# The decay's and the rate's low-rank products, issued together in the two halves of the array's rows

## The chip, the cores and the metric

The kernel runs on one core of a Trainium2 chip. Its time is the device time of one execution in microseconds (us); of several runs the median is given. The engines are TensorE (PE in the profile, PEld for its weight loads), VectorE (DVE), ScalarE (ACT), GpSimd (POOL) and SyncE (SP), which issues most of the DMAs. Each has its own queue of instructions, runs it in order, and waits on semaphores for the others.

## The reference, cut to what matters

One layer of a hybrid decoder, on 512 prompt tokens and 8 sequences of 4 sample tokens, 544 tokens in all. A combined projection feeds three branches: a gated MLP, an RWKV-7 recurrence with 16 heads of 64 channels, and cross-attention to a memory. The branches are projected, gated and summed, and an MLP follows. What is changed lies in the RWKV branch, where the projections `wl` and `al` (64 channels each) give the decay and the rate of each of 1024 channels:

```python
w_log = -jax.nn.softplus(-(p['w0'] + jnp.tanh(wl) @ p['w_w2']).astype(f32)) - 0.5
decay = jnp.exp(-jnp.exp(w_log))
a = jax.nn.sigmoid((p['a0'] + al @ p['w_a2']).astype(f32))
...
kk = heads(kz * p['k_k'])
kk = kk * lax.rsqrt(jnp.sum(kk * kk, axis=-1, keepdims=True) + 1e-12)
k = kz.astype(f32) * (1.0 + (a - 1.0) * p['k_a'].astype(f32))
...
y, S = wkv7_scan(r_h, heads(decay), k_h, v_h, -kk, kk * a_h, wkv0.astype(f32))
```

## The kernel before, in words

Channels lie on the 128 partitions and the 544 tokens along the free axis. The big products, which the text calls the trunk, are tiles of 128 output features (`trunk`, L500): eight tiles of input features with three products each, of a weight and an activation that are each split into two float32r parts. A weight half comes by DMA (L190), ACT makes its first part (`whi`, L198) and DVE its second (`wlo`, L211), two halves ahead of their use. Everything else on PE is float32, and for each such product that the program names the trace shows two passes (weight loads and matmuls).

The recurrence is done in chunks of 32 tokens, for a pair of heads (128 channels) at a time: eight pairs, `pr` 0 to 7, two of them to a group. `prep_pair` prepares a pair. The decay's product (L842) takes the 64 rows of `la` that hold `tanh(wl)`, the rate's (L849) the other 64 rows; each goes over 544 tokens as 256 and 288 columns. ACT makes them `t_L` and `t_a` by a tanh (L844, L850) and squares the keys (L843). DVE rescales `t_L` (L852), PE sums the squares by head (L859), DVE scans `t_L` (L865), PE spreads the norms (L878), DVE forms the rows `AG..e` and `AG..o` (L904, L905), and PE multiplies the rows of each chunk (L923, L925), in two quarters of the array that share neither rows nor columns. When both pairs of a group are there, POOL inverts the chunks' triangles (`inv_stream`): DVE transposes them in (L1005), POOL runs a chain of 60 instructions (L1010, L1012), DVE sets the diagonal (L1015) and transposes out (L1017, L1019), and PE uses them first at L1026. After that the recurrence itself (L1067 to L1106) steps from chunk to chunk, and `out_stream` finishes the values (`y_f` at L1158, the product with wg at L543).

Streams of such pieces are dealt out by a planner (`Sched`), which knows rough times of the instructions and no overlap on PE: a piece follows when its stream's priority and its results allow, and the trunk fills what is left. A piece ends at a `yield`; DONE means that the stream's next piece waits for this one's results. The plan fixes the order of each engine's instructions. An accumulator `pst` has two PSUM banks of 512 columns; three of them serve this stage, and `take` and `pt_free` get and return one.

Of the kernel before, what the change touches and what calls it, by code (L numbers as in the profile page):

```python
# [39 lines left out]
class Dry:  # L40
    """Stands in for a device object of which only the calls matter."""
# [17 lines left out]
class Shape:  # L59
    """Stands in for a tile or a view of one while the order of the program is planned."""  # L60
# [41 lines left out]
class Model:  # L102
    """Rough times of the engines' instructions: from these the order of the program is planned. An
    instruction waits for its engine and for what its own piece of the program has written."""
# [58 lines left out]
class Plan:  # L163
    """The order in which the streams' pieces follow each other, and the choices on the way: found
    on the model, then replayed."""
# [8 lines left out]
class Weights:  # L174
    """Streams the weight halves [128, 4 x 128] in the order of their use, splitting each into the
    two float32r parts two halves ahead of its use."""
# [17 lines left out]
    def high(self):  # L194
        """The first part of the next half."""
        hi = self.pool.tile([128, 512], F32R, name="whi")
        raw = self.pool.tile([128, 512], F32, name="wraw") if self.dry else self.raw.pop(self.nhi)
        self.nc.scalar.copy(hi, raw)  # L198
        self.his[self.nhi] = hi, raw
        self.nhi += 1  # L200
# [31 lines left out]
    def advance(self, lo):  # L232
        """Keeps the parts AHEAD halves ahead: first the one, later the other."""
        if not self.dry:
            self.load_to(self.nhi + 1)
            if self.nhi >= len(self.plan.seq) + (lo and self.nlo < self.nhi):
                return
        elif self.nhi >= HALVES_ALL + (lo and self.nlo < self.nhi):
            return
        else:  # L240
            self.nc.model.side = True
        if lo:
            self.low()
            if not self.dry:
                self.load_to(self.nhi + RAWB)
        else:
            self.high()
        if self.dry:
            self.nc.model.side = False
# [32 lines left out]
class Sched:  # L282
    """Interleaves generators by priority. What a generator yields says when its next piece should
    follow: at once (NOW), when the results of this one are there (DONE), not before a time has passed
    (AFTER, or PAUSE if without them), or when a flag has been set: ("need", flag) after the results, too, ("when", flag) without them. A run ends when only streams of the background
    are left."""
# [58 lines left out]
def body(nc, tc, io, plan, dry, dbg=None):  # L345
# [16 lines left out]
    def psum(n):  # L362
        """n accumulators of two banks and single banks for the rest."""
        if pools:
            pools["small"].close()
            pools["big"].close()
        pools["big"], pools["small"] = ExitStack(), ExitStack()
        pools["t"] = pools["big"].enter_context(tc.tile_pool(name="ps_t", bufs=1, space=PSUM))
        pools["c"] = pools["small"].enter_context(tc.tile_pool(name="ps_c", bufs=8 - 2 * n, space=PSUM))
        slots[:] = [0.0] * n  # L370

    def pt():
        """The accumulator that is free first, until pt_free."""
# [107 lines left out]
    def flush():  # L481
        """The next one of the late parts of each tile."""
# [7 lines left out]
    def trunk(key, xh, xl, evac, halves=HALVES, needs=None):  # L490
        """128 output features: eight tiles of 128 input features, three products each. evac may return
        its later parts, one or a list, and whether the accumulator is free without them."""
# [29 lines left out]
    def trunk_stream():  # L522
        """The trunk's tiles: the first job whose condition holds, of the queues in their order."""
# [13 lines left out]
    def sum_bc(lhsT, rhs, ps=None):  # L537
        """[128, 544] = lhsT^T rhs in float32."""
# [11 lines left out]
    def sum_cols(out, t, blocks=range(5)):  # L550
        """The sum over the features, over D, a token to a partition: out [128, 5]."""
# [3 lines left out]
    def spread(out, recb, blocks=range(5)):  # L555
        """The blocks' factors [128, 5, 128], one for each token, to every partition."""
# [19 lines left out]
    # =====================================================================================  # L576
    # Phase 0: memory keys and values, first norm
    # =====================================================================================
# [104 lines left out]
    # =====================================================================================  # L683
    # Phase 2: RWKV
    # =====================================================================================
# [30 lines left out]
    def shift(ps, j, t, after=None):  # L716
        """Mixes each row with the one before; two parts, the second one to be called later."""
# [66 lines left out]
    def ev_gelu(dst):  # L784
        """Twice the gelu."""
# [36 lines left out]
    def prep_pair(g, pi, d):  # L822
# [16 lines left out]
        # decay and rate of each channel  # L839
        ps, sl = yield from take()  # L840
        for o, s, n in HALVES:
            PE.matmul(ps[:, o:o + n], lhsT=wa2[0:64], rhs=la[0:64, s:s + n], start=True, stop=True)  # L842
        S.activation(sq, k, AF.Square, scale=vc("kk", pr))  # L843
        S.activation(L, ps[:, 256:800], AF.Tanh, scale=0.5, bias=hv[:, pr:pr + 1])  # L844
        pt_free(sl)
        yield DONE
        ps, sl = yield from take()
        for o, s, n in HALVES:
            PE.matmul(ps[:, o:o + n], lhsT=wa2[64:128], rhs=la[64:128, s:s + n], start=True, stop=True)  # L849
        S.activation(a, ps[:, 256:800], AF.Tanh, scale=0.5, bias=hv[:, 8 + pr:9 + pr])  # L850
        pt_free(sl)
# [3 lines left out]
        # 1 / |kk|^2 by token and head  # L855
# [33 lines left out]
        # decayed rows  # L889
# [28 lines left out]
        # products of the rows of a chunk  # L918
# [24 lines left out]
        # the sample rows' hats wait in DRAM for the sample stage  # L943
# [21 lines left out]
    def fill(g, half):  # L965
        """Values and token-major keys of half the chunks, into the tiles that the recurrence reads."""
# [29 lines left out]
    def inv_stream():  # L996
        for g in range(4):
# [3 lines left out]
            # inverses of the unit lower triangles, one matrix to a partition  # L1001
# [107 lines left out]
    def group_norm(Yt, n):  # L1109
        """Yt [128, n, 64] in place: zero mean and unit variance over the last axis."""  # L1110
# [53 lines left out]
    def slot_512():  # L1164
        """A bank that the piece at hand also empties."""
        ps, sl = yield from take()
        pt_free(sl)
        return ps[:, 0:512]
# [135 lines left out]
    # =====================================================================================  # L1304
    # Phase 3: spatial gating, attention, the branches' projections
    # =====================================================================================
# [8 lines left out]
    def pair(first, k, name):  # L1315
        """The two float32r parts of feature tile k, in the first or the second set of buffers."""
# [80 lines left out]
    def gate_in(first):  # L1397
        """Token-major values."""
# [31 lines left out]
    def layer_norm(first):  # L1430
        """The values are twice the reference's, and so is what stands under the root four times it."""
# [92 lines left out]
    def cache_stream():  # L1524
        """The cached heads [128, 2 x 256], split into their float32r parts ahead of their use."""
# [24 lines left out]
    def sample_att():  # L1550
# [4 lines left out]
        # sel[8 h + 4 l + t, 16 + 4 h + t] = 1: adds the rows of the two parts (l) of the queries  # L1555
        sel = sb(sa, [32, 48], "sel")
        # for each half of the sum, the queries (or weights) of head h of sequence b at column 24 + 32 (4 b + h),
        # in two parts, and zeros between, so that 32 columns from 8 h before them put their products at rows 8 h
        qp = sb(sa, [128, 2, 1048], "qp", F32R)

        def parts_to(x, k):
            """The two parts of x [128, 8, 4, 4] (b h t)."""
# [22 lines left out]
        def products(name, half):  # L1585
            """Four sequences' products with their four queries or weights, whose two parts stand side by
            side (rows 8 h + 4 l + t), as rows of SBUF."""
# [79 lines left out]
    def prompt_att():  # L1667
# [14 lines left out]
        for h in range(4):  # L1682
# [11 lines left out]
            # scores and softmax  # L1694
# [67 lines left out]
    # =====================================================================================  # L1762
    # Phase 4: output projection, MLP, final norm
    # =====================================================================================
# [13 lines left out]
    def square(tot, j):  # L1778
        """Adds x1[j] squared to tot."""
# [27 lines left out]
    def ev_up(c, j):  # L1807
        """The square of what is above zero; the norm's factor, which is above zero, comes after w_down."""
# [40 lines left out]
    def last_two():  # L1849
        """The last two tiles, the first tokens of both before the others of both, so that the end of the  # L1850
        first ones' work runs beside the others' products."""
# [76 lines left out]
    def final_stream(half):  # L1928
        """The final norm and the output of the first or of the other tokens."""
# [142 lines left out]
```

## Time and profile before

| | |
|---|---|
| runs shown | 1496.42, 1493.64, 1495.51 us, median 1495.51 |
| span of the profiled execution | 1494.6 us, 0.9 below that median |
| PE busy | 1419.6 us, 95% |
| DVE, ACT, POOL busy | 64%, 42%, 29% |
| mean granted clock of TensorE | 0.981 of full speed |
| the changed products | 64 passes between 102 and 535 us |

A row of the timeline has the start in us, the duration in us, the engine, line and operation, the tile written and those read, the shape and the count of instructions merged; in brackets stands how long the engine was idle before it, and for whom. A duration on PE reaches from an instruction's start to its modelled end, and successive matmuls overlap; what one costs is read from the distance between starts. Rows of the groups of instructions end in busy time, mean ns of one, and the idle time before them.

### The profile page before, as it was taken

The page shows a single profiled execution, that of the slowest core. Times are in us where ns is not written, and L with a number is a line of the kernel's source. Part 1 is how long each engine was busy: PE and PEld are TensorE (multiplying, and loading weights), DVE is VectorE, ACT ScalarE, POOL GpSimd, SP SyncE. Part 2 cuts the span into 40 slices and gives each one's busy share as a digit, 9 for nine tenths or more (in the row PEclk, how much of TensorE's full clock was granted, in tenths as well). Part 3 has the DMA queues.
Part 4 walks back from the last instruction along what each step waited for, and adds up shares of the span by engine and source line. Part 5 has one row for each costly group of instructions (what it writes and reads, how often), then busy time and mean ns, then how long its engine had stood idle before and what let it go on. Part 6 is the DMA issues. An engine that isn't in the chain of part 4 may idle for free. (4 is left out here: it accounts for less than half of the span.)

```text
span 1494.6 us, 31352 instructions
## 1 busy us (share of the span) xinstructions
PE 1419.6 (95%) x12436; PEld 1326.7 (89%) x12436; DVE 952.5 (64%) x1639; ACT 630.0 (42%) x1549; POOL 426.1 (29%) x485
## 2 busy tenths in 40 slices
PE   7899989998998899999998998999999999999997
PEld 7899988887888788878888897889999999999996
DVE  6747877757778777577657667664564454544544
ACT  4434335655565365555424145542334323323222
POOL 5320281452107503620333333322110020120222
PEclk9999999999999999999999999999999999999998
DMA  6632222222312322242467557633422222223222
GB/s 223 192 112 83 91 65 71 70 68 81 107 60 69 112 83 90 89 148 93 153 221 279 180 174 247 224 126 119 156 85 86 89 96 85 91 79 97 88 86 82
DMA packets 106499, 177.45 MB, mean 119 GB/s; under 512 B 15440, under 2 KB 29008, under 8 KB 106352
## 3 DMA queue, kind: packets, MB, share of 16 engines
q1 hardware_dynamic: 104512, 172.06, 36.0%
q8 instruction: 98, 1.61, 0.4%
q0 software_dynamic: 640, 2.23, 0.4%
q10 hardware_dynamic: 1200, 1.16, 0.2%
q14 instruction: 49, 0.40, 0.1%
HBM read 147.89 MB, written 27.51 MB: 117 GB/s over the span
## 5 line engine op out<-in xcount | busy, mean ns | idle before, releaser
L211 DVE TENSOR_TENSOR wlo<-wraw,whi 128x512 fp32r<-128x512 f32 x372 | 309.1, 848 | 44.1 <-ACT whi L198 41.5
L198 ACT CAST whi<-wraw 128x512 fp32r<-128x512 f32 x372 | 224.0, 618 | 159.3 <-PE pst L500 102.0
L500 PE MATMUL pst<-hh,whi 128*128 128x256 f32 (+1 forms) x1184 | 275.2, 314 | 9.6 <-DVE Em L985 4.5
L500 PE MATMUL pst<-hh,wlo 128*128 128x256 f32 (+1 forms) x1184 | 247.1, 290 | 2.2 <-DVE wlo L211 2.2
L500 PE MATMUL pst<-hl,whi 128*128 128x256 f32 (+1 forms) x1184 | 246.5, 290 | 0.0
L500 PEld LDWEIGHTS pst<-hh,whi 128*128 128x128 f32 x1184 | 189.2, 191 | 30.1 <-issue 10.6
L500 PEld LDWEIGHTS pst<-hh,wlo 128*128 128x128 f32 x1184 | 192.0, 191 | 2.7 <-DVE wlo L211 2.7
L500 PEld LDWEIGHTS pst<-hl,whi 128*128 128x128 f32 x1184 | 192.8, 191 | 0.0
L1837 POOL TENSOR_TENSOR x<-x,dn 128x544 f32<-128x544 f32 x24 | 41.7, 1737 | 292.8 <-DVE dn L1835 292.8
L500 PE MATMUL pst<-gh,whi 128*128 128x256 f32 (+1 forms) x512 | 106.4, 289 | 0.0
L500 PE MATMUL pst<-gl,whi 128*128 128x256 f32 (+1 forms) x512 | 105.5, 287 | 0.0
L500 PE MATMUL pst<-gh,wlo 128*128 128x256 f32 (+1 forms) x512 | 105.1, 287 | 0.0
L1090 ACT COPY YU<-psc 32x64 f32<-32x64 f32 x256 | 51.7, 202 | 76.7 <-DVE Xe L1087 71.3
L500 PE MATMUL pst<-y_h,whi 128*128 128x256 f32 (+1 forms) x384 | 83.1, 298 | 0.3 <-ACT pr L1710 0.3
L500 PEld LDWEIGHTS pst<-gl,whi 128*128 128x128 f32 x512 | 82.7, 189 | 0.0
L500 PEld LDWEIGHTS pst<-gh,whi 128*128 128x128 f32 x512 | 81.9, 188 | 0.1
L500 PEld LDWEIGHTS pst<-gh,wlo 128*128 128x128 f32 x512 | 81.7, 188 | 0.0
L1010 POOL TENSOR_TENSOR Tt<-Xinv 128x30 f32<-128x30 f32 (+14 forms) x120 | 67.9, 566 | 45.9 <-DVE Xinv L1005 37.1
L500 PE MATMUL pst<-y_l,whi 128*128 128x256 f32 (+1 forms) x384 | 79.7, 289 | 0.0
L500 PE MATMUL pst<-y_h,wlo 128*128 128x256 f32 (+1 forms) x384 | 79.6, 289 | 0.0
L1012 POOL TENSOR_TENSOR Xinv<-Xinv,Tt 128x30 f32<-128x30 f32 (+14 forms) x120 | 75.2, 627 | 9.4
L1813 DVE TENSOR_TENSOR ff_r<-ff_r,pst 128x544 f32<-128x544 f32 x32 | 23.1, 720 | 81.4 <-ACT ff_r L1812 81.4
(411 smaller groups left out, 3149.5 us busy)
## 6 DMA issues: line engine op xcount, KB each, us to landing
wraw<-win SPq DMA_DIRECT2D x148, 256.0 KB, 2.7
wraw<-up SPq DMA_DIRECT2D x64, 256.0 KB, 2.7
wraw<-down SPq DMA_DIRECT2D x64, 256.0 KB, 2.7
wraw<-br SPq DMA_DIRECT2D x48, 256.0 KB, 3.3
craw<-ck SPq DMA_DIRECT2D x32, 256.0 KB, 4.3
craw<-cv SPq DMA_DIRECT2D x32, 256.0 KB, 3.6
gz_d<-gzs SPq DMA_DIRECT2D x24, 272.0 KB, 2.9
gt<-gz_d SPq DMA_DIRECT2D x24, 272.0 KB, 3.0
```

The costliest lines, as they stand in the source:

```text
L198: self.nc.scalar.copy(hi, raw)
L211: (self.nc.gpsimd if pool else self.nc.vector).tensor_tensor(lo, raw, hi, op=ALU.subtract)
L500: PE.matmul(ps[:, o:o + n], lhsT=w[:, c], rhs=x[kt][:, s:s + n], start=kt == 0 and i == 0, stop=kt == KT - 1 and i == 2)
L1010: G.tensor_tensor(t3, X[:, j + 1:32, j:j + 1].to_broadcast([128, n, j]), X[:, j:j + 1, 0:j].to_broadcast([128, n, j]), op=ALU.mult)
L1012: G.tensor_tensor(X[:, j + 1:32, 0:j], X[:, j + 1:32, 0:j], t3, op=ALU.add)
L1090: S.copy(YU[q + 32 * pi:q + 32 * pi + 32, c, :], p3[q:q + 32, pi, :])
L1813: V.tensor_tensor(r, r, ps[:, 256:800], op=ALU.mult)
L1837: G.tensor_tensor(x1[j], x1[j], t, op=ALU.add)
```

## The change: both products in one piece, half of the tokens at a time

The two pieces for the decay and the rate become two pieces for the first and the second 272 tokens. Each issues the decay's product in rows 0 to 63 of the array and the rate's in rows 64 to 127, both over all 128 columns, into the two banks of one accumulator, and then two tanhs of 272 columns. The Square comes behind the tanhs of the first piece. The rescaling of `t_L` and `k1` become a piece of their own, behind a DONE. All other edits replace comments by blank lines, which keeps the line numbers.

```diff
-        for o, s, n in HALVES:
-            PE.matmul(ps[:, o:o + n], lhsT=wa2[0:64], rhs=la[0:64, s:s + n], start=True, stop=True)
-        S.activation(sq, k, AF.Square, scale=vc("kk", pr))
-        S.activation(L, ps[:, 256:800], AF.Tanh, scale=0.5, bias=hv[:, pr:pr + 1])
-        pt_free(sl)
-        yield DONE
-        ps, sl = yield from take()
-        for o, s, n in HALVES:
-            PE.matmul(ps[:, o:o + n], lhsT=wa2[64:128], rhs=la[64:128, s:s + n], start=True, stop=True)
-        S.activation(a, ps[:, 256:800], AF.Tanh, scale=0.5, bias=hv[:, 8 + pr:9 + pr])
-        pt_free(sl)
+        for half in range(2):
+            ps, sl = yield from take()
+            h = slice(272 * half, 272 * half + 272)
+            for q in (0, 64):
+                PE.matmul(ps[:, 8 * q:8 * q + 272], lhsT=wa2[q:q + 64], rhs=la[q:q + 64, h], start=True, stop=True)
+            S.activation(L[:, h], ps[:, 0:272], AF.Tanh, scale=0.5, bias=hv[:, pr:pr + 1])
+            S.activation(a[:, h], ps[:, 512:784], AF.Tanh, scale=0.5, bias=hv[:, 8 + pr:9 + pr])
+            pt_free(sl)
+            if half == 0:
+                S.activation(sq, k, AF.Square, scale=vc("kk", pr))
+            yield DONE
         V.tensor_scalar(L, L, -DECAY_C, -DECAY_C, op0=ALU.mult, op1=ALU.add)
         S.activation(k1, k, AF.Copy, scale=hv[:, 24 + pr:25 + pr])
         yield DONE
```

The plan comes out differently from the first pair on. On PE, at the first pair's decay (`la` holds both inputs, `wa` the pair's weights, `hh` and `whi` are the trunk's):

```order
 L500 MATMUL pst<-hh_95,wlo 128x256
 L500 MATMUL pst<-hh_95,wlo 128x288
-L842 MATMUL pst<-la,wa_1051 128x256
-L842 MATMUL pst<-la,wa_1051 128x288
+L845 MATMUL pst<-la,wa_1051 128x272 x2
 L500 MATMUL pst<-hh_96,whi 128x256
 L500 MATMUL pst<-hh_96,whi 128x288
```

Two products of the trunk's size become two of half that size, and the second such row stands 18 trunk instructions further on, where L849 stood 12 further on.

On DVE, at the end of the first group's inversion (`Xinv` is the inverse, `AG1o` the rows of the third pair), before the change:

```order
L211 TENSOR_TENSOR wlo<-wraw,whi 128x512
L1015 COPY Xinv<-qmask 128x32
L904 TENSOR_TENSOR AG1o<-t_r,PP 64x16x32
L905 SCALAR_TENSOR_TENSOR AG1o<-t_L,PP 64x16x32
L1017 STREAM_TRANSPOSE Tt<-Xinv 128x32x32
```

On the same engine and at the same place after it:

```order
L904 TENSOR_TENSOR AG1o<-t_r,PP 64x16x32
L905 SCALAR_TENSOR_TENSOR AG1o<-t_L,PP 64x16x32
L1015 COPY Xinv<-qmask 128x32
L211 TENSOR_TENSOR wlo<-wraw,whi 128x512
L1017 STREAM_TRANSPOSE Tt<-Xinv 128x32x32
```

L1015, which needs the last of POOL's chain, moves from ahead of the rows to behind them, and a weight part of the trunk comes to stand behind it.

On DVE, at the end of the second group's inversion (L1086, L1087 and L1102 belong to the recurrence's step), before the change:

```order
L1015 COPY Xinv<-qmask 128x32
L1102 TENSOR_TENSOR Xe<-psc,SP 64x2x64
L1102 TENSOR_TENSOR Xo<-psc,SP 64x2x64
L1017 STREAM_TRANSPOSE Tt<-Xinv 128x32x32
L211 TENSOR_TENSOR wlo<-wraw,whi 128x512
```

There after it (`gzs` is a gelu of the trunk's):

```order
L1015 COPY Xinv<-qmask 128x32
L1017 STREAM_TRANSPOSE Tt<-Xinv 128x32x32
L794 SCALAR_TENSOR_TENSOR gzs<-gzs,pst 128x544
L1019 STREAM_TRANSPOSE CT_1028<-Xinv 128x32x32
L211 TENSOR_TENSOR wlo<-wraw,whi 128x512
L1086 COPY Xo<-psc 32x2x64
```

The step's additions (L1102) move ahead of L1015, and its copies stand behind the transpositions.

Counted along PE's order: from the odd pair's last chunk product to the first L1026 there are 288, 258, 342 and 282 trunk instructions in the four groups before, and 294, 240, 330 and 282 after. From the first decay product to L859 there are 30, 30, 30, 18, 24, 24, 12 and 18 before, and 48, 36, 54, 24, 30, 24, 48 and 30 after. Behind the last product with wg (L543 of `out_stream`) 198 trunk instructions with w_in are left before, 162 after. The array's shape (rows x columns) changes 523 times from one product to the next before, 529 times after.

## Rows read from the trace of the kernel before

**Rows 1.** The page: busy times, and TensorE's granted clock in 40 slices, in tenths.

```profile
PE 1419.6 (95%) x12436; PEld 1326.7 (89%) x12436; DVE 952.5 (64%) x1639; ACT 630.0 (42%) x1549; POOL 426.1 (29%) x485
...
PEclk9999999999999999999999999999999999999998
```

**Rows 2.** Stretches: length, PE, PEld, DVE, ACT, POOL busy (instructions), PEclk, DMA share, GB/s.

```profile
100.00:200.00 100.00, 98.45 (x839) 93.21 (x838) 76.54 (x149) 40.98 (x101) 26.37 (x36) 1.00 0.25 78
200.00:300.00 100.00, 92.13 (x994) 82.78 (x992) 72.86 (x151) 49.66 (x152) 40.92 (x63) 0.95 0.22 69
...
500.00:600.00 100.00, 95.03 (x1059) 83.91 (x1058) 78.22 (x157) 56.52 (x166) 25.35 (x41) 0.98 0.30 97
...
1000.00:1100.00 100.00, 100.00 (x805) 100.00 (x805) 50.48 (x65) 32.92 (x57) 21.94 (x16) 1.00 0.41 128
```

**Rows 3.** Groups of PE's instructions, 100 to 540 us: the decay's and the rate's.

```profile
L842 PE MATMUL pst<-la,wa 64*128 64x256 f32 (+1 forms) x32 | 9.4, 415 | 0.0
L849 PE MATMUL pst<-la,wa 64*128 64x256 f32 (+1 forms) x32 | 9.4, 415 | 0.0
```

**Rows 4.** Timeline of PE around the first decay product.

```profile
101.88 0.41 PE L500 MATMUL pst<-hh,wlo 128*128 128x256 f32 x2
102.22 1.18 PE L842 MATMUL pst<-la,wa 64*128 64x256 f32 x4
...
103.69 0.41 PE L500 MATMUL pst<-hl,whi 128*128 128x256 f32 x2
```

**Rows 5.** Timeline of PE around a float32 product on the full array.

```profile
124.71 0.41 PE L500 MATMUL pst<-hh,wlo 128*128 128x256 f32 x2
124.96 1.08 PE L543 MATMUL pst<-t_x,bones 128*128 128x256 f32 x4
...
126.13 0.41 PE L500 MATMUL pst<-hl,whi 128*128 128x256 f32 x2
```

**Rows 6.** Timeline of PE at the first chunk products.

```profile
126.72 0.27 PE L923 MATMUL pst<-AG0e,BK 64*64 64x64 f32 x1
126.72 0.27 PE L925 MATMUL pst<-AG0o,BK 64*64 64x64 f32 x1
126.83 0.22 PE L923 MATMUL pst<-AG0e,BK 64*64 64x64 f32 x1
...
126.88 0.22 PE L923 MATMUL pst<-AG0e,BK 64*64 64x64 f32 x1
```

**Rows 7.** Timeline of PE at the third pair's chunk products.

```profile
216.95 0.32 PE L923 MATMUL pst<-AG1e,BK 64*64 64x64 f32 x2
221.14 0.36 PE L925 MATMUL pst<-AG1o,BK 64*64 64x64 f32 x1 [3.87 <-DVE AG1o L905]
221.14 0.36 PE L923 MATMUL pst<-AG1e,BK 64*64 64x64 f32 x1
```

**Rows 8.** Groups of ACT's instructions: a tanh, an exponential and a copy out of PSUM.

```profile
L844 ACT ACTIVATE t_L<-pst,hv 128x544 f32<-128x544 f32 x8 | 5.7, 709 | 4.7 <-PE pst L842 4.6
L1710 ACT ACTIVATE pr<-pst,nm 128x256 f32<-128x256 f32 x16 | 7.3, 471 | 1.3 <-DVE sms L1627 0.9 <-DVE nm L1705 0.4
L625 ACT COPY rstm<-psc x1: 372/372/372, 21.7 to 21.7; 128x256 f32<-128x256 f32 x1
```

**Rows 9.** Timeline of DVE at the end of the first inversion.

```profile
219.46 0.20 DVE L1015 COPY Xinv<-qmask 128x32 f32<-128x32 f32 x1 [6.59 <-POOL Xinv L1012]
```

**Rows 10.** A stretch behind that wait, columns as in rows 2.

```profile
220.50:230.70 10.20, 8.04 (x128) 7.50 (x130) 8.27 (x9) 1.99 (x4) 0.85 (x3) 0.50 0.25 80
```

**Rows 11.** Timelines of DVE and PE at the end of the second inversion.

```profile
321.99 2.17 DVE L1017 STREAM_TRANSPOSE Tt<-Xinv 128x1024 f32<-128x1024 f32 x1
...
326.25 1.20 PE L1026 MATMUL pst<-CT,Tt 32*32 32x32 f32 x64
```

**Rows 12.** Timelines of DVE and PE at the end of the third inversion.

```profile
503.82 2.08 DVE L1017 STREAM_TRANSPOSE Tt<-Xinv 128x1024 f32<-128x1024 f32 x1
...
506.50 1.54 PE L543 MATMUL pst<-t_x,bones 128*128 128x256 f32 x4 [2.47 <-DVE y_f L1158]
```

More of the change, by code (lines that the diff above doesn't have):

```diff
@@ L838, in prep_pair @@
         k1 = sb(rp, [128, T], "t_n")
-        ps, sl = yield from take()
-        for o, s, n in HALVES:
-            PE.matmul(ps[:, o:o + n], lhsT=wa2[0:64], rhs=la[0:64, s:s + n], start=True, stop=True)
-        S.activation(sq, k, AF.Square, scale=vc("kk", pr))
-        S.activation(L, ps[:, 256:800], AF.Tanh, scale=0.5, bias=hv[:, pr:pr + 1])
-        pt_free(sl)
-        yield DONE
-        ps, sl = yield from take()
-        for o, s, n in HALVES:
-            PE.matmul(ps[:, o:o + n], lhsT=wa2[64:128], rhs=la[64:128, s:s + n], start=True, stop=True)
-        S.activation(a, ps[:, 256:800], AF.Tanh, scale=0.5, bias=hv[:, 8 + pr:9 + pr])
-        pt_free(sl)
+        for half in range(2):
[9 more added lines that the diff above has]
+            yield DONE
         V.tensor_scalar(L, L, -DECAY_C, -DECAY_C, op0=ALU.mult, op1=ALU.add)
```

## The prediction

> **What bounds the kernel now.** I read the page first: TensorE is busy 95% of the span and holds its high clock nearly throughout [rows 1]. A table by stretches shows where that is not so: behind 1000 us PE is full, while in the stretch of the change, 100 to 600 us, it is busy 92 to 98 us of each 100 and the clock drops here and there; ACT is at 41 to 57% [rows 2]. So a microsecond of PE work is worth a microsecond, unless PE stands shortly behind it for another engine. Next the groups of instructions: the two products that change are 32 passes each, a float32 product being two passes, and PE never waits ahead of them [rows 3]. Then the timeline around one, for its price. Last the timelines of the ends of the triangles' inversions, the places where PE and DVE wait for POOL, because a saving ahead of such a wait may be lost in it.
>
> **What is removed.** A pair of passes of the trunk takes 0.25 us (124.71 to 124.96, [rows 5]). The trunk's pair of 101.88 is thus over at 102.13, the pair of 103.69 stands 0.25 us behind one that in full flow would have begun at 103.44, and the decay's product takes 1.31 us of PE [rows 4]. The same columns on the full array take 0.92 us (124.96 to 126.13 less 0.25, [rows 5]), which is the streaming of four passes over 2 x 544 columns, 0.85 ns each. The other 0.39 us is what two changes of the array's shape cost, about 0.2 us each. There are 16 such groups, eight pairs with a decay and a rate each.
>
> **What is put in its place.** Again 16 groups, each with two products of 272 columns in the two halves of the rows. If the halves run side by side a group streams 0.46 us instead of 0.92 and keeps the 0.39: 0.85 us, and 16 x 0.46 = 7.4 us of PE go away. No row of before shows two products that share the columns of the array and differ in rows alone. The nearest are the chunk products, which differ in both: two begin together at 126.72, and the next ones of L923 at 126.83 and 126.88; alone a pass of 64 columns streams 54 ns by the 0.85 ns above, which is all that lies between couples, so both are at work at once [rows 6]. Bounds: all of the 0.46 us by these rows; nothing at all if the halves exclude each other, the decay's own price [rows 4]; and a loss of up to 0.39 us for each group (6.2 us) if going from one half to the other cost what a change of shape does. I take the 7.4, since the chunk products are the nearest kind.
>
> Do two passes of one product, issued ahead of the other's, hold it up? At 216.95 both passes of L923 start, and L925 stands until 221.14, when a pass of the next L923 starts with it, ahead of L925's own second pass [rows 7]. So a product's passes are issued one behind the other, and still two products overlap pass by pass. The Trainium skill ("TensorE: Matmul & The Clock Gate", Part 3, What overlaps and what doesn't) says that matmuls keep the program's order in start and end; by that the second half would start with the first half's second pass, and three of four passes would remain. The trace speaks against it with the row of 221.14. It is a rival below.
>
> **What moves.** Both tanhs now come in two parts of 272 columns. A tanh of 544 takes 709 ns; of 256 columns out of PSUM ACT needs 372 ns for a copy and 471 for an exponential with a sum [rows 8], so 272 lie between 0.39 and 0.49. With 0.43, four take 1.72 us instead of 1.42: 8 x 0.3 = 2.4 us more on ACT, which is idle about half of the time here [rows 2] and hides it; without that cover they would cost these 2.4 us. The Square moves behind the first two tanhs, and its reader L859 now stands 48 trunk instructions behind the first group instead of 30 in the first pair. The rescaling of L and the activation into k1 get a stop of their own behind the second pair of tanhs: one stop more in each pair's preparation. On DVE the scan queues behind the rescaling as before. No DMA is added; the preparation's loads and stores move with their pieces in SP's queue. The trunk fills the longer preparation, as it filled the shorter one: in PE's order the last product with wg stands 36 trunk instructions later, with 162 of w_in's left behind it instead of 198, so the filler does not run out, and if it did that would cost up to 36 x 0.125 = 4.5 us.
>
> The planner deals all pieces of the stage anew. Along PE's order 529 products have another shape than the one ahead instead of 523: 6 x 0.2 = 1.2 us lost.
>
> **What the waits give back.** An inversion is a chain on POOL that starts when the odd pair's chunk products are masked, and L1026 on PE needs its end. Between these, PE has 294, 240, 330 and 282 trunk instructions in the four groups instead of 288, 258, 342 and 282, and in the first three also two of the cheaper groups (0.92 us less). First group: 6 x 0.125 - 0.92 = 0.17 us less work on PE, and PE stands there already: DVE stands 6.59 us for POOL at L1015, and behind it AG1o, for which PE stands 3.87 us [rows 7, 9]. Now AG1o comes ahead of L1015, which moves the wait to L1026 and doesn't end it. Lost: 0.2 us. Second: 18 x 0.125 + 0.92 = 3.2 us less, against a cover of 326.25 - 324.16 = 2.1 us that L1026 has behind the end of L1017 [rows 11]. Lost: 1.1 us. Third: 12 x 0.125 + 0.92 = 2.4 us less, where PE now stands 2.47 us at L543 behind y_f, which in DVE's queue comes behind L1017 [rows 12]; in the new order y_f stands right behind L1015, ahead of L1017, so this wait may go. Between 0 and 2.4; I take 1.2. Fourth: nothing.
>
> **The sum.** -7.4 + 1.2 + 0.2 + 1.1 + 1.2 = -3.7 us. The profiled execution has a span of 1494.6 us; the runs' median is 1495.51, 0.9 us around it, and nothing at the ends changes: 1494.6 - 3.7 + 0.9 = 1491.8 us.
>
> **Rivals.** (a) Forecast, 1491.8, for a waits' redistribution of 3 us either way: 0.47.
> (b) The halves run one behind the other, or half so. Then the change doesn't do what it says: no group gets cheaper, only order and shapes change. 1495.5 + 1.2, less or more some tenths at the inversions: 1496.9. With three of four passes left, 16 x 0.23 = 3.7 us go, and 1.2 + 1.3 come back: 1494.3. For it: no row has halves with shared columns. Against: [rows 6, 7]. Together 0.18, within the measurement's reach.
> (c) Slower: the second inversion gets what the first one has. DVE stands at L1015 with nothing but a copy and a transposition ahead of the gelu, a weight part and the chain's copies L1086 and L1087, PE runs dry behind them and the clock falls. The first inversion's price is 3.87 us of wait and 10.2 us at the lower of the clock's two levels, 1.2 GHz [rows 7, 10], half of which is 5.1 us: 9.0, of which 1.1 is in the sum. 1491.8 + 7.9 = 1499.7. It decides once that place costs more than 6.5 us. For it: L1026 has a cover of 2.1 us and loses 3.2. Against: no fall of the clock there today, and the trunk has weights split ahead. 0.19, other new holds of the same kind along the new order included.
> (d) All is kept and the wait of 3.87 us goes too, because with AG1o ahead of L1015 the trunk reaches past POOL's end: 1495.5 - 7.4 + 1.2 - 3.9 = 1485.4. Against: L1026 follows L923 after 6 trunk instructions. 0.16.
>
> **How the numbers follow.** A measurement of this kernel can tell about 0.2%, 3 us: faster is under 1492.5, slower above 1498.5. Faster: three quarters of (a), 0.35, all of (d), 0.16, a little of (b), 0.03: 0.54. Same: 0.12 of (a), 0.14 of (b), 0.01 of (c): 0.27. Slower: 0.18 of (c) and 0.01 of (b): 0.19. The range goes from a little under (d) to a little above (c), 1484 to 1501.
>
> **What would show it.** L845: 64 passes of 272 columns in couples that begin within some ns, a group 0.85 us between trunk pairs. If the second half starts a whole pass or more after the first, (b) holds. PE's wait at L925 near 221 gone, one at L1026 in its place. At the second inversion, a DVE wait at L1015 of about 3 us; with a fall of the clock there, (c). What would make the forecast wrong is above all PE's waits between 100 and 1000 us, which the new order deals anew.

## The result, and the profile after

The changed kernel takes 1507.5 us (median of 7 runs, 1501.0 to 1510.0) where the kernel before takes 1496.4 (7 runs, 1493.6 to 1500.1): 1.006 of it, 95% interval 1.004 to 1.008. It is slower by some 9 us by this ratio (11 by the medians); the forecast was 1491.8, and the time lies above the upper end of the range, 1501. The profiled execution of the changed kernel took 1502.75 us with a span of 1501.0; it is one of the quicker ones, so its rows show 6.4 us of the loss (1501.0 - 1494.6).

The first two lines are of the page of the changed kernel (TensorE's busy tenths and granted clock in 40 slices, answering to [rows 1]), the others its table by stretches, columns as in [rows 2].

```profile
PE   7899998989998899999998999999999999999997
PEclk9999998999999999899999999999999999999998
```

```profile
100.00:200.00 100.00, 98.16 (x857) 93.47 (x856) 73.63 (x143) 43.22 (x108) 21.18 (x29) 1.00 0.28 85
200.00:300.00 100.00, 93.34 (x1000) 84.25 (x1000) 72.40 (x147) 47.49 (x146) 36.49 (x57) 0.93 0.23 72
500.00:600.00 100.00, 93.11 (x1020) 82.24 (x1021) 78.42 (x157) 53.97 (x160) 26.18 (x39) 0.97 0.30 95
600.00:700.00 100.00, 93.29 (x958) 79.48 (x956) 59.91 (x122) 50.94 (x165) 29.93 (x45) 0.95 0.35 110
1000.00:1100.00 100.00, 99.39 (x797) 99.00 (x796) 50.72 (x74) 32.27 (x62) 20.84 (x15) 1.00 0.42 124
```

Behind 1000 us nothing has changed: the last 3500 matmuls take 449.8 us before and 449.5 after. The loss lies ahead of that. The changed instructions themselves are cheaper, as forecast: the timeline of TensorE around the first group (answering to [rows 4]).

```profile
102.17 0.41 PE L500 MATMUL pst<-hh,wlo 128*128 128x256 f32 x2
102.52 0.73 PE L845 MATMUL pst<-la,wa 64*128 64x272 f32 x4
103.17 0.52 PE L500 MATMUL pst<-hh,whi 128*128 128x256 f32 x2
103.53 0.41 PE L500 MATMUL pst<-hl,whi 128*128 128x256 f32 x2
```

From the end of the trunk's pair (102.17 + 0.25) to the point at which the next would have begun in full flow (103.53 - 0.25) are 0.86 us where it was 1.31. The four passes begin in couples, 5 to 7 ns between the halves and, in 15 of the 16 groups, 0.33 us between the couples. 16 x 0.45 = 7.2 us of TensorE's work are gone.

What came in their place is seen in the waits. TensorE between 95 and 1000 us, the first lines of each list: who waits, on whom, us in total, times, longest. First before, then the changed kernel.

```profile
PE psc L1094 <- DVE Xe L1087: 5.2, 5, 2.9
PE pst L500 <- DVE Em L985: 4.5, 4, 1.4
PE psc L1067 <- DVE Xe L1102: 4.2, 4, 2.6
PE pst L925 <- DVE AG1o L905: 3.9, 1, 3.9
```

```profile
PE psc L1094 <- DVE Xe L1087: 8.5, 8, 2.9
PE pst L500 <- DVE Em L985: 7.5, 5, 2.1
PE pst L1026 <- DVE t_vb L914: 6.4, 1, 6.4
```

Summed over all matmuls but the first, idle times above 0.3 us grew from 57.8 to 64.2 us. The other 7 us of the balance (6.4 = -7 + 6.4 + 7) are in none of these lists. What they consist of (rows at the lower clock, small pauses, changes of shape) was not taken apart.

The largest new wait is at the end of the first inversion. Timelines of POOL, DVE and PE there, answering to [rows 7, 9], and behind them the stretch of the lower clock, answering to [rows 10].

```profile
183.67 0.25 POOL L1010 TENSOR_TENSOR Tt<-Xinv 128x30 f32<-128x30 f32 x1 [6.45 <-DVE Xinv L1005]
```

```profile
225.47 0.20 DVE L1015 COPY Xinv<-qmask 128x32 f32<-128x32 f32 x1 [5.45 <-POOL Xinv L1012]
```

```profile
223.11 0.27 PE L923 MATMUL pst<-AG1e,BK 64*64 64x64 f32 x1
223.12 0.27 PE L925 MATMUL pst<-AG1o,BK 64*64 64x64 f32 x1
...
231.65 1.56 PE L1026 MATMUL pst<-CT,Tt 32*32 32x32 f32 x51 [6.44 <-DVE t_vb L914]
```

```profile
227.50:237.70 10.20, 6.05 (x98) 5.77 (x100) 7.44 (x8) 1.37 (x3) 0.00 (x0) 0.50 0.30 104
```

The wait has left L925 and stands at L1026, with 10.2 us at the lower clock as before. It takes the place of 3.87 + 0.62 + 0.90 us at the same inversion before, so it is longer by 1 us. It ends with L914 on DVE, which empties the accumulator that L1026 needs and stands behind L1015 and both transpositions there. The end of POOL's chain, for which L1015 waits, comes 6.0 us later (225.47 against 219.46), because the chain began later: 183.67, where the same row of before is

```profile
178.27 0.25 POOL L1010 TENSOR_TENSOR Tt<-Xinv 128x30 f32<-128x30 f32 x1 [6.48 <-DVE Xinv L1005]
```

At the third inversion the wait at L543 behind y_f [rows 12] has not gone but changed its owner:

```profile
506.24 1.16 PE L543 MATMUL pst<-t_x,bones 128*128 128x256 f32 x4 [1.99 <-DVE Xinv L1015]
```

### The profile page after: what moved, and what is told of

It reads as the page before. It is cut to its first block, busy times and chain, and to the rows that moved or that the text cites. A ratio compares the mean times of both kernels' runs of the same rounds, so it can differ in the third digit from the quotient of the medians.

```text
span 1501.0 us, 31387 instructions
## 1 busy us (share of the span) xinstructions
PE 1419.1 (95%) x12436; PEld 1323.1 (88%) x12436; DVE 959.8 (64%) x1639; ACT 632.6 (42%) x1565; POOL 422.5 (28%) x485
```

## Experiments

Runs of different batches are compared by their ratio to the kernel before, which ran beside each batch (medians 1498.96 in the first, then 1498.76, 1497.43 and 1499.39). For a whole set of runs two more numbers can be read from the list of spans and mean granted clocks: "lost" is the mean of span x (1 - clock), the rest is span x clock. The lower level, 1.2 GHz, is a clock of 0.50. A fall counts as lost inside a wait too, where TensorE has nothing to do, so only the span decides, and the two show where to look.

**First batch: order and overlap apart.** Run 1 lets the planner work on the old pieces and issues the new ones:

```diff
+        if dry:
+            ps, sl = yield from take()
...
+        else:
+            for half in range(2):
+                ps, sl = yield from take()
+                h = slice(272 * half, 272 * half + 272)
+                for q in (0, 64):
+                    PE.matmul(ps[:, 8 * q:8 * q + 272], lhsT=wa2[q:q + 64], rhs=la[q:q + 64, h], start=True, stop=True)
...
+                pt_free(sl)
+                if half == 0:
+                    yield DONE
...
```

Under `if dry:` stand the two pieces of before; the Square stays ahead of the first tanhs, and the decay's scaling and k1 stay in the second piece.

> The products of the changed kernel (two pieces of 272 tokens, decay and rate in the two row halves) put where the products of the kernel before stood; the order of the whole program is planned on the old pieces, so everything else stands as before. Theory O (the products' overlap saves its 7.2 us, 16 groups x 0.45, and the loss comes from the new order of the program): 1489 us, 1487.5 to 1491. Rival I (TensorE's saving comes back as waits whatever the order, since the preparation's chain and not TensorE sets the pace): 1495 to 1498. Rival S (the split in halves itself hurts, by longer chains of tanh or more accumulator pieces): 1500 to 1508.

Measured: 1496.54 us, 0.9986 (0.9973 to 0.9999). Some 2 us of the 7.2 arrive: the time lies in Rival I's range or, by the ratio (0.9986 of 1496.4, from which the ranges were set, is 1494.3), between it and Theory O's. Theory O's size is wrong, and S is out.

Run 2 is the reverse, under the same two branches: planned on the changed kernel's pieces, issuing the old products.

> The order of the changed kernel, planned on its pieces, but in the pieces the old products: the decay's 256 and 288 tokens in the first, the rate's in the second, both in series in one row half. Theory O: the changed kernel's 1507.5 us plus the lost overlap of 7.2 us = 1514.7, 1512 to 1516. Rival I: TensorE's time is not what counts there either, so within 2 us of the changed kernel, 1505.5 to 1509.5.

Measured: 1509.47 us, 1.0072 (1.0056 to 1.0088). The new order alone costs 10.8 us, and in it too the overlap gives back only some 2 us (1.0072 to 1.006; the intervals overlap), again a time in Rival I's range. Its list of waits is the changed kernel's, not that of before, so these waits belong to the order:

```profile
PE psc L1109 <- DVE Xe L1102: 8.0, 9, 3.0
PE pst L1041 <- DVE t_vb L929: 7.2, 1, 7.2
PE pst L500 <- DVE Em L1000: 5.8, 4, 1.7
```

(L1109 and L1041 are L1094 and L1026, 15 lines on.) Runs 3 and 4 move the order of the kernel before by other means, a `yield DONE` ahead of the decay's scaling, and `GAP = 0.23`.

> The kernel before with one more piece border (the scaling of the decay and the copy k1 as a piece of their own, behind an extra wait for results), as the changed kernel has it, and nothing else; the order is planned anew. If this border is what spoils the order: 1511 to 1516, the changed kernel's time with serial products. If the new order is an accident of the plan that no part of the change owns: anything from 1490 to 1512, and then not near the run above (more than 3 us from it).

Measured: 1506.41 us, 1.0052 (1.0037 to 1.0068). That is slower, but less than the 1511 to 1516 by which this border would own the loss.

> Control: the kernel before, with the planner's allowance between a piece's results and its next piece at 0.23 instead of 0.22; no instruction is other than before, only the planned order moves. If the order found by the plan scatters by several us for any small cause: 1490 to 1508, at least 3 us from 1496.4. If plans that are nearly the same are worth the same: 1495 to 1498, and a definite part of the change must be looked for.

Measured: 1507.62 us, 1.0059 (1.004 to 1.0077). A hundredth of a microsecond in a constant of the planner, with no instruction other than before, costs as much as the whole change.

**Second batch: is TensorE's work on the path, and is it the first hold?** Run 5 doubles the products (`for o, s, n in HALVES * (1 if dry else 2)`).

> The kernel before in its own order, but each of the decay's and the rate's products is issued twice in series into the same accumulator, which adds TensorE work (16 groups x 0.78 us = 12.5 us) and nothing else. If every microsecond of TensorE's work in this stage is a microsecond of the time: before + 12.5. If most of what is saved or added there is taken up by waits whose ends other engines set (2 of 7.2 us arrived when the products were overlapped in this order): before + 3 to + 7.

Measured: 1511.67 us, 1.0078 (1.0057 to 1.0098), +11.7 us of 12.5. Work that is added counts nearly in full, which speaks against waits as a general cushion and against Rival I. It does not show that TensorE's work alone is the path, since the longer products also lengthen the preparation's chain in which they stand. At the first inversion's end there is one, though:

```profile
227.68 0.27 PE L925 MATMUL pst<-AG1o,BK 64*64 64x64 f32 x1 [1.54 <-DVE AG1o L905]
```

The 3.87 us of [rows 7] have shrunk to 1.54; in run 1 they grew:

```profile
221.81 0.37 PE L941 MATMUL pst<-AG1o,BK 64*64 64x64 f32 x1 [5.05 <-DVE AG1o L921]
```

Runs 6 and 7 permute the planner's list of pieces between the first inversion's end and the middle of the second group's preparation (a list of 171 indices, not shown); an accumulator that is still taken is replaced by the one that has been free longest. The text calls it the second inversion and the odd pair's products; it is the first, and the products are pair 2's.

> The overlapped products in the order of the kernel before, and one stretch of the order changed by hand: the end of the second inversion (VectorE's copy of the diagonal and the transposes, L1015 to L1019, and TensorE's products L1026) stands behind the odd pair's last chunk products (L925) instead of between them, with trunk rows drawn forward, and the foreground behind it stands up to three trunk rows later until the third inversion. In the overlapped kernel TensorE waits there 5.05 + 0.64 + 0.92 us and its granted clock then stands at 0.50 for 10.2 us, in which it loses some 4.4 us. If that hold is what takes up the overlap's saving: 5 to 10 us under the overlapped kernel without the move, 1487 to 1491 where before is 1497. If the wait only moves to the next place that the recurrence's chain sets: within 2 us of it.

Measured: 1496.5 us, 0.9982 (0.9969 to 0.9994).

> The kernel before with its own products in series, and the same stretch of the order changed as in the run above. The hold there is 3.87 + 0.62 + 0.90 us and 10.2 us at a granted clock of 0.50. If the hold counts: 4 to 8 us under before. If waits take up the overlap's saving, the run above lies under this one by more than the 2 us that the overlap was worth without the move: 3.5 to 7 us; if the overlap is worth some 2 us wherever it stands, 2 us.

Measured: 1499.97 us, 1.0004 (0.9991 to 1.0018). The hold and its fall of the clock are gone from both traces, and neither is faster: in run 6 a trunk row, which waited 1.26 us near 297 us in run 1, now waits for an accumulator that DVE empties late.

```profile
294.22 0.65 PE L514 MATMUL pst<-hh,whi 128*128 128x256 f32 x2 [3.11 <-DVE Em L1015]
```

So the wait moved on, as the rival said, though the new hand-out of the accumulators may have a part in where it went. Run 6 lies 3.3 us under run 7 by the ratios, between the two readings of run 7 (2, and 3.5 to 7). Run 8 is the second control, `GAP = 0.21`.

> Control: the kernel before with the planner's allowance at 0.21 instead of 0.22; no instruction changes, the order is planned anew. If the order of the kernel before is one of the best of a wide scatter, as the run with 0.23 (+8.7 us) says: again some 4 to 11 us slower than before. If 0.23 was an accident to one side: within 2 us of before.

Measured: 1496.25 us, 0.9989 (0.9975 to 1.0003). Orders scatter, and not every other order is worse.

**Third batch: TensorE kept busy.** Run 9 adds products to run 1:

```diff
+    def warm(ps, n):
+        if not dry:
+            for _ in range(n):
+                PE.matmul(ps[:, 0:256], lhsT=hh[0][:, 0:128], rhs=hh[1][:, 0:256], start=True, stop=True)
...
+            if pr == 2 and c8 == 0:
+                warm(ps, 32)
```

> The overlapped products in the order of the kernel before, and at the one place where TensorE then waits longest (5.05 us at 221.8 us, before pair 2's chunk products, L925; the granted clock stands at 0.50 for 10.2 us from 221.7) 32 products of 256 columns whose results are written over, some 3.5 us by the trunk's 0.12 us each, so that TensorE works in a time in which it would wait. They compute nothing that is used. Theory C (the overlap's saving arrives at full clock, and what the lower clock then takes is 2 to 5 us of it): the fall at 221 us is gone or short, and the time is 3 to 5 us under the overlapped kernel without them, 1492 to 1493.5 where before is 1498.8. Rival (the clock's falls are the same share of any run, or the added products delay what follows): no gain, 1496 to 1500.

Measured: 1498.25 us, 1.0003 (0.999 to 1.0016). No gain; Theory C was wrong here. TensorE in run 9:

```profile
215.70 3.95 PE L825 MATMUL pst<-hh,hh 128*128 128x256 f32 x32
221.44 0.27 PE L948 MATMUL pst<-AG1o,BK 64*64 64x64 f32 x1 [1.53 <-DVE AG1o L926]
224.07 1.20 PE L1049 MATMUL pst<-CT,Tt 32*32 32x32 f32 x64 [1.49 <-DVE Tt L1040]
226.90 0.82 PE L500 MATMUL pst<-hh,whi 128*128 128x256 f32 x2 [1.63 <-DVE t_vb L935]
```

and the last two of these rows in run 1, where L1042 is run 9's L1049 (the row ahead of them is the one at 221.81 above):

```profile
224.41 1.92 PE L1042 MATMUL pst<-CT,Tt 32*32 32x32 f32 x64 [0.64 <-DVE Tt L1033]
227.25 0.82 PE L500 MATMUL pst<-hh,whi 128*128 128x256 f32 x2 [0.92 <-DVE t_vb L930]
```

Up to 227 us DVE sets the pace: at full clock TensorE only waits more. The fall came anyway, at 225.4 for 6.8 us instead of 221.7 for 10.2, so it ended at the same time, and what it costs is what lies behind 227. Run 10 adds five more places, with `warm(ps[:, 128:512], ...)` in the chain's pieces and `warm(ps, 16)` ahead of pair 6's product.

> As the run above, with such products at five more places of stage 2 where TensorE waits 1.2 to 2.9 us in the overlapped kernel (before L1067 of group 0's chunk 9 and of group 1's chunk 2, L1094 of group 1's chunk 5 and of group 2's chunk 15, and pair 6's product at L543): 8, 18, 8, 20 and 16 of them. Theory C: the falls at 297, 365, 396, 515 and 624.5 us (3.4 to 6.8 us each, of which about half is lost) go as well, another 5 to 10 us, 1484 to 1489. Rival: each product delays the chain behind it, and it is slower than the run above.

Measured: 1491.38 us, 0.996 (0.9946 to 0.9974): the fastest version here, by 6 us under the kernel before and by 15 under the changed one (0.996 against 1.006). Against run 9, which ran beside it and differs by these five places alone, its mean span is 7.0 us shorter, and its mean time lost to the clock falls by nearly as much, from 27.3 to 20.9 us. The falls at 297, 365, 396 and 624.5 us are gone; those near 224 and 511 us stayed, and one at 453 is new. At one of the six places the products do not stand in the wait but behind it:

```profile
501.78 2.16 PE L825 MATMUL pst<-hh,hh 128*128 128x256 f32 x16 [2.41 <-DVE y_f L1185]
```

Two of the stretches, in run 1 and in run 10, columns as in [rows 2]:

```profile
355.00:385.00 30.00, 27.02 (x251) 24.33 (x249) 22.73 (x44) 14.42 (x47) 8.16 (x4) 0.89 0.31 98
...
615.00:640.00 25.00, 22.14 (x290) 19.98 (x290) 15.94 (x28) 10.73 (x30) 10.11 (x19) 0.86 0.20 59
```

```profile
355.00:385.00 30.00, 29.06 (x284) 26.21 (x283) 25.44 (x50) 15.76 (x51) 8.17 (x4) 1.00 0.35 112
...
615.00:640.00 25.00, 23.16 (x320) 20.88 (x319) 20.40 (x36) 11.58 (x31) 10.71 (x15) 1.00 0.24 75
```

Runs 11 and 12 are about the order again: run 8's `GAP = 0.21` with run 1's edit, and the changed kernel with the loop's `yield DONE` under `if half == 0`.

> The overlapped products in the order planned with the allowance at 0.21 on the old pieces (1496.25 us with the products in series). If the overlap is worth 5 to 7.5 us at full clock and loses 2 to 4.5 us of that to the clock in every order, as in the three orders so far: 1492 to 1495. If it is worth its 7.2 us in an order with fewer falls: 1489.

Measured: 1494.86 us, 0.9978 (0.9967 to 0.9989): the first range, 1.6 us under run 8 by the ratios.

> The changed kernel without its extra piece border (the decay's scaling and k1 stay in the second piece), the order planned anew. If the border is what spoils the order (it cost the kernel before 7.7 us by itself): 1491 to 1497. If orders scatter whatever moved them (so far -2, +8, +9 and, with products in series, +11 us against before): anywhere between 1490 and 1507.

Measured: 1500.31 us, 1.0021 (1.001 to 1.0032). Without the border some 6 of the change's 9 us are gone (1.006 against 1.0021). This is a new draw of the order too, so the border and the draw are not told apart.

**Fourth batch: the overlap's worth with TensorE busy.** Run 13 has run 10's added products in the kernel before, run 14 such products at five waits of the changed kernel.

> The kernel before with its own products in series and its own order, and the added products at the same six places as in the run with the overlap (1491.4 us there, 0.996 of before). If the lower clock is what took the overlap's saving, the two with TensorE kept busy differ by the overlap's own 5 to 7.2 us: 1496.5 to 1498.5, hardly under before (1497.4). If the added products are what gained the 6 us, and the overlap still gives only its 2: 1493 to 1494.

Measured: 1497.07 us, 0.9988 (0.9976 to 1.0). The time lies in the first range, but the kernel before was 2 us slower in this batch than the 1497.4 from which the ranges were set; 0.9988 of 1497.4 is 1495.6, between the two ranges. So this run alone does not decide.

> The changed kernel in its own order, with such added products at five of its own waits (40 before L1026 of group 0, 14 before L1094 of group 0's chunk 13, 20 before L1094 of group 2's chunk 14, 14 before pair 6's product at L543 and 14 before pair 3's at L543), whose falls of the clock at 227.5, 507, 524 and 626.8 us last 27 us, half of them lost. If the clock took 4.6 us of the overlap's saving in this order: 1501 to 1504 where the changed kernel is 1507.5. If the order's waits, which VectorE and GpSimd set, are all that counts: 1506 to 1509.

Measured: 1504.74 us, 1.0044 (1.0027 to 1.006): 2 us less than the changed kernel, within the intervals. The run can't tell the two readings apart, because at three of the five places the products do not fill the wait. By the trace they wait themselves, for the accumulator that they write, and run behind the wait as work that is added:

```profile
233.09 7.46 PE L825 MATMUL pst<-hh,hh 128*128 128x256 f32 x40 [7.70 <-DVE t_vb L921]
```

The others of this kind are the two at L543. The falls at 524.4 and 626.8 us are gone; those near 228 and 510 us stayed, and one at 317 is new.

The pairs that differ by the overlap alone (mean us over all their runs; series, then overlapped; of the kernel before, its runs in all four batches):

| order | span | lost to the clock | rest |
|---|---|---|---|
| of before (run 1) | 1496.7, 1495.0 | 26.4, 29.7 | 1470.3, 1465.4 |
| of the changed kernel (run 2) | 1507.8, 1504.6 | 26.1, 30.7 | 1481.6, 1473.9 |
| moved by hand (runs 7, 6) | 1498.3, 1494.1 | 23.0, 24.9 | 1475.3, 1469.2 |
| GAP 0.21 (runs 8, 11) | 1495.2, 1493.2 | 20.8, 23.9 | 1474.4, 1469.3 |
| of before, kept busy (runs 13, 10) | 1495.1, 1489.5 | 20.7, 20.9 | 1474.4, 1468.7 |

In every order the rest falls by 4.9 to 7.7 us, near the 7.2 of work. In the first four 1.9 to 4.6 us of it come back at the lower clock, and 1.7 to 4.2 us of span remain. Where products were added at six waits nothing comes back, and 5.6 us remain: 3.9 us more than in the same order without (95% interval of that difference about 1.3 to 6.5, from the runs' scatter). Runs 10 and 13 are of different batches, though. With each run taken against the kernel before of its own batch it is 3.2 us by the means (0.3 to 6.2), and 2 us by the ratios, with an interval of some 3.4 us either way. So that the added products free more of the overlap's saving is likely, not shown.

## Why the prediction was wrong

**What was right.** The overlap and its price: the groups at 0.86 us against 0.85, the couples 5 to 7 ns apart; rival (b) is out. ACT carries its extra parts (tanhs of 487 and 481 ns, at the upper of the estimate's bounds of 0.39 and 0.49, so 4.1 us more on ACT and not 2.4); DVE's idle time for the tanh of `t_L` is 4.9 us in all against 3.8, and run 1, which has the same parts in the old order, isn't slower for them. The wait at L925 went, and one at L1026 took its place.

**The step that failed: "What the waits give back".** With the line on shapes ahead of it, it judged the new order by the trunk instructions between the odd pair's chunk products and L1026, and by six shape changes, 1.2 + 0.2 + 1.1 + 1.2 = 3.7 us. Run 2 prices the order at 10.8 us. In the table they stand in the rest (1481.6 against 1470.3), not in what the clock takes (26.1 against 26.4). The step looked at the ends of the inversions alone; the waits that grew most, at L1094 behind the copies of the recurrence's step (L1087) and at trunk rows behind DVE's L985, lie elsewhere. It also took no account of when an inversion begins. The start of POOL's chain for the second group, before and after:

```profile
282.08 0.25 POOL L1010 TENSOR_TENSOR Tt<-Xinv 128x30 f32<-128x30 f32 x1 [9.39 <-DVE Xinv L1005]
```

```profile
292.30 0.25 POOL L1010 TENSOR_TENSOR Tt<-Xinv 128x30 f32<-128x30 f32 x1 [9.50 <-DVE Xinv L1005]
```

It comes 10.2 us later. Most of that is the trunk, which the new order puts ahead: TensorE has begun 1188 trunk instructions by then, before 1110, and 78 x 0.125 are 9.8 us. That work is gone from what comes later, so the lateness is not itself a loss. Nor does the start go with the time in the runs whose order was planned anew: 289.6 us with the border alone (1.0052), 291.6 with GAP 0.23 (1.0059) and 296.3 in the changed order with serial products (1.0072) are late and slow, but 286.3 with GAP 0.21 is late and not slow (0.9989), and 279.9 without the border is early and slower (1.0021). The fourth group's chain starts at 583.9 us in the changed kernel and at 584.2 in the kernel before, with 2487 trunk instructions begun in both. So the saving of the overlap is spent by then (idle times above 0.3 us from 90 us on: 30.0 us against 25.5), and the 6.4 us of the profiles are lost behind it, ahead of some 1000 us.

**The size that was off: the 7.4 us.** As work of TensorE they are there. The first paragraph took "a microsecond of PE work is worth a microsecond"; in an unchanged order 2 us of 7 arrive (run 1). Two things are seen to take from the rest: a hold whose end POOL and DVE set (3.87 to 5.05 us, above), and the lower clock, whose mean is longer in each of the four overlapped kernels whose waits were left idle (by 1.9 to 4.6 us; the 1.9 lies within the runs' scatter). In run 1 the clock fell at 296.8 us behind waits of 1.17 and 1.26 us within some 3 us, where before stood 0.98 and 1.25 us and it did not fall; in the serial runs 7 and 8 it fell near there too (298.9 and 300.7 us). That saved work turns into idle time and so into falls is argued. That falls cost time is supported by run 10 against run 9, where the span fell by as much as what was lost to the clock. Run 13 speaks less clearly: against the kernel before it lost 5.7 us less to the clock and gained 1.6 us of span. Run 9 had a shorter fall and no gain. How much of the missing 5 us the clock has taken stays open.

**The rivals.** (c) had the sign and, with 1499.7, set the upper part of the range, but its mechanism did not come: at the second inversion DVE waits 0.23 and 1.19 us, not about 3.

```profile
330.50 0.20 DVE L1015 COPY Xinv<-qmask 128x32 f32<-128x32 f32 x1 [0.23 <-POOL Xinv L1012]
331.89 2.15 DVE L1017 STREAM_TRANSPOSE Tt<-Xinv 128x1024 f32<-128x1024 f32 x1 [1.19 <-POOL Xinv L1012]
```

Its threshold of 6.5 us does not follow from the sum either: 1498.5 - 1491.8 and the 1.1 us already in it make 7.8. (d) did not happen: L1026 inherited the wait. The third inversion's wait, taken at half its 2.4 us, stayed at 1.99. The chance of 0.19 for slower was too low because the planner's scatter was priced at "3 us either way": the five new draws of the order here (runs 2, 3, 4, 8 and, with the overlap in it, 12) lie between 0.9989 and 1.0072 of before.

**What stays open.** The cause inside the order: which of its waits are worth how much of the 10.8 us. Moving one by hand moved its wait on (runs 6, 7). Each trace is one execution: in the profiles of runs 1, 9, 10 and 13, which keep the old order, and of the kernel before, the stretch from the fourth group's chain to the end takes 909.3 to 915.1 us, and 917.1 in the changed kernel.

## What to carry to other kernels

Where a planner deals out the whole program, an edit of one piece is two changes: its own, and a new draw of the order. Time them apart, by planning on the old pieces and issuing the new ones, and learn the scatter of the draw first by moving a constant that touches no instruction. A saving on an engine that is 95% busy is worth its microseconds only where that engine isn't about to wait. Filling waits with work that is thrown away removed falls of the clock here; with the overlap it gave some 4 us (run 10 against run 1), in the kernel before some 2, at the edge of its interval (run 13). The trace has to show that such work stands in the wait: work that needs the very buffer for which the engine waits runs behind it (run 14).

## What the runs showed of the hardware that was not expected

Two float32 products in the two halves of the array's rows that share all its columns overlap pass by pass: couples begin 5 to 7 ns apart, and four passes of 272 columns take the time of two (0.86 us for the group with its shape changes, 1.31 in series). Keeping TensorE at work inside a wait does not always hold the clock: 32 products of 3.95 us ahead of a wait of 1.53 us still left 6.8 us at 0.50 (run 9), while with 18 and 20 products in what had been waits of 2.6 and 2.9 us (run 1) the falls there were gone (run 10).
